# Exits of the mLSTM and RWKV stages inside their plans, and float32 products with 64 columns in column halves

## The chip, the cores and the metric

The kernel runs on one core of a Trainium2 chip. Its time is the device time of one execution in microseconds (us); of several runs the median counts. Engines: PE is TensorE, DVE is VectorE, ACT is ScalarE, POOL is GpSimd, SP issues most DMAs. A traced execution gives the times of single instructions, in us from the start of its span.

## The reference

A stack of four layers (mLSTM, RWKV7, Retention, mLSTM) on 256 tokens of width 1024; around each mixer stand two half-step SwiGLU networks:

```python
for layer in range(DEPTH):
    g = norm_g[layer]
    h = swiglu_ffn(rms_norm(x, g[0]), ffn_w_gu[layer, 0], ffn_w_down[layer, 0])
    x = x + HALF_STEP * rms_norm(h, g[1])
    h = mixer[layer % 3](rms_norm(x, g[2]), ...)
    x = x + rms_norm(h, g[3])
    h = swiglu_ffn(rms_norm(x, g[4]), ffn_w_gu[layer, 1], ffn_w_down[layer, 1])
    x = x + HALF_STEP * rms_norm(h, g[5])
```

mLSTM computes for each of 4 heads gated scores of q and k times v, normalises and gates the result y, and multiplies it by w_out. RWKV7 runs, per head of 64, the recurrence `S = S*w + (S a) b^T + v k^T`, `y = S r`, normalises y, adds `sum(r k r_k) v`, gates it and multiplies by w_out. All of it is float32.

## The kernel before

The 256 tokens are two tiles (t = 0, 1) of 128 partitions; x[0] and x[1] (in the order: x_88, x_89) stay in SBUF. The weights come as 345 units of 1 MB. Each unit is split into a high part (`hi`, copied by ACT, L127) and a low part (`lo`, subtracted by DVE or POOL, L135), and every dense product is three products at reduced precision, `hi*xh + lo*xh + hi*xl` (`mm3`, L334 to L340). This splitting is called prep below. So that the next units are ready, preps are put in between the other work of ACT, DVE and POOL.

The net is a row of twelve stages. A stage's body ends with its output products: `acc[t]` (two PSUM halves of 512 columns for each tile) adds up w_out's units times the transposed and split head outputs `hT`; a unit makes 12 products per tile (`down_steps`). Then come, for each tile, `residual` (ACT squares L268, DVE L270, a chain of small DVE operations for the reciprocal root, and x itself, L276) and `x_transpose` (8 PE transposes of x, L292; DVE scales them, L298; ACT makes `xh`, L299; DVE makes `xl`, L302), and then the next stage's first products, `head.mm`.

`boundary` writes this passage in a fixed order: the stage gives back a list `tail` of functions f(t); all f(0) go first, then preps and the residual of tile 0, then the f(1), with the x transposes of tile 0 ahead of the last of them, then the residual of tile 1 and `head.mm`. The mLSTM stage leaves the output products of heads 1 to 3 to the tail, with the transposes and splits (L1046, L1063, L1067) of heads 2 and 3; RWKV leaves those of its last two groups for tile 1.

The bodies of mLSTM and RWKV are put in order by `Plan`, a list scheduler that runs while the program is built. A body is a set of chains (Python generators) that yield an engine, a cost in ns, and whether a PSUM bank is taken. Plan takes the chain whose step can start first, after adding to each chain's time its constant from `PUT_OFF`; it assumes four PSUM banks and one port that DVE's two-input operations share with POOL. Nothing of this is decided on the chip: there every engine follows its own written order and waits on semaphores.

In RWKV, `solve` (L1959), `right` (L1826) and `outputs` (L2009, L2012, L2014) multiply float32 matrices of 128 x 128 by 64 moving columns (two in L2014), four products to a group. `by_rows` (L346) issues other small products in two halves of 64 partitions. `lora2` makes the second LoRA products for w and for a, each with 64 rows. `s.slot` and `s.heads` only choose slices.

## Time and profile before

| | us |
|---|---|
| median of 3 runs (lowest, highest) | 2175.19 (2174.14, 2177.9) |
| profiled execution | 2175.98 |
| its span | 2174.2 |
| mLSTM bodies and exits (about) | 196 to 327, 1860 to 1994 |
| RWKV | 660 to 956 |
| mean granted clock of PE | 0.983 |

A line of the trace's timeline gives start, length, engine, line of the program, operation, output and inputs (partitions x elements), a count, and in brackets the idle time of the engine before it and what ended it. Matmuls overlap, so the distance between two starts is the pitch of one, not its length. PEclk is the clock granted to PE, 1.0 being full.

### The profile page before, as it was taken

How to read it: one execution, taken by the hardware profiler on the slowest of the kernel's cores; microseconds unless marked ns; L12 is line 12 of the kernel's file. 1: busy time of each engine (PE TensorE's matmuls, PEld its weight loads, DVE VectorE, ACT ScalarE, POOL GpSimd, SP SyncE). 2: the span in 40 equal slices, each digit the busy share in tenths (PEclk: the TensorE clock that was granted, in tenths of full speed). 3: DMA queues.
4: the chain of work that ended last, by engine and by line, in shares of the span. 5: the costliest groups of instructions: out<-in, count | busy, mean ns of one | idle time of the engine just before them, and what ended most of it. 6: DMA issues, size and time to landing. Idle time of an engine off the chain costs nothing.

```text
span 2174.2 us, 38941 instructions
## 1 busy us (share of the span) xinstructions
PE 2091.4 (96%) x16136; PEld 1976.0 (91%) x16136; DVE 1492.2 (69%) x2234; ACT 1112.9 (51%) x1804; POOL 356.2 (16%) x615
## 2 busy tenths in 40 slices
PE   8999989999998999879999999999999999998998
PEld 8999879999997988879999999998999999887997
DVE  6766777667666787677677668556766766757765
ACT  5545655445445754345445445444544554655543
POOL 2001421002000466730001003211000100252000
PEclk9999999999999999889999999999999999999999
DMA  7553245555552320136546555554654555234651
GB/s 278 214 201 136 108 171 211 211 191 195 216 192 98 124 76 31 55 145 251 195 156 244 204 194 194 175 175 146 230 204 169 217 211 194 100 117 191 233 205 68
DMA packets 56226, 376.46 MB, mean 173 GB/s; under 512 B 7144, under 2 KB 8808, under 8 KB 11888
## 3 DMA queue, kind: packets, MB, share of 16 engines
q1 hardware_dynamic: 55472, 372.59, 46.9%
q8 instruction: 127, 2.08, 0.4%
q10 hardware_dynamic: 576, 1.38, 0.2%
q14 instruction: 51, 0.42, 0.1%
HBM read 372.89 MB, written 1.05 MB: 172 GB/s over the span
## 4 chain that ended last, share of the span: by engine, by line
PE 82%; DVE 11%; ACT 3%; issue 2%; POOL 1%; DMA 1%; DVEq 0%; SPq 0%; ACTq 0%; POOLq 0%
PE mm L338 14%; PE mm L340 14%; PE mm L339 14%; PE acc L336 7%; PE acc L334 7%; PE acc L335 7%; PE mm L334 4%; PE mm L335 4%; PE mm L336 4%; DVE lo L135 3%; DVE s L864 1%; ACT hi L127 1%; DVE s L270 1%; DVE x L276 1%; PE acc L1440 1%
## 5 line engine op out<-in xcount | busy, mean ns | idle before, releaser
L135 DVE TENSOR_TENSOR lo<-raw,hi 128x1024 fp32r<-128x1024 f32 (+1 forms) x700 | 810.3, 1200 | 188.6 <-ACT hi L127 186.2
L127 ACT ACTIVATE hi<-raw 128x1024 fp32r<-128x1024 f32 (+1 forms) x766 | 697.7, 964 | 116.5 <-issue 57.0
L338 PE MATMUL mm<-xh,hi 128*128 128x256 f32 x2688 | 743.1, 276 | 0.0
L339 PE MATMUL mm<-xl,hi 128*128 128x256 f32 x2688 | 741.3, 276 | 0.0
L340 PE MATMUL mm<-xh,lo 128*128 128x256 f32 x2688 | 741.2, 276 | 0.0
L339 PEld LDWEIGHTS mm<-xl,hi 128*128 128x128 f32 x2688 | 518.0, 193 | 1.7
L338 PEld LDWEIGHTS mm<-xh,hi 128*128 128x128 f32 x2688 | 518.0, 193 | 1.7
L340 PEld LDWEIGHTS mm<-xh,lo 128*128 128x128 f32 x2688 | 518.1, 193 | 0.0
L336 PE MATMUL acc<-hi,s 128*128 128x512 f32 x864 | 331.3, 383 | 7.4 <-DVE s L1067 6.3
L334 PE MATMUL acc<-hi,s 128*128 128x512 f32 x864 | 333.9, 387 | 4.3 <-ACT s L1063 2.3
L335 PE MATMUL acc<-lo,s 128*128 128x512 f32 x864 | 330.0, 382 | 0.0
L571 ACT ACTIVATE s<-s 128x256 f32<-128x256 f32 x152 | 63.6, 419 | 431.9 <-DVE s L569 431.9
L334 PE MATMUL mm<-hi,xh 128*128 128x256 f32 x960 | 268.8, 280 | 5.3 <-ACT xh L1392 5.3
L335 PE MATMUL mm<-lo,xh 128*128 128x256 f32 x960 | 265.4, 276 | 0.9 <-DVE lo L135 0.9
L336 PE MATMUL mm<-hi,xl 128*128 128x256 f32 x960 | 265.2, 276 | 0.0
L336 PEld LDWEIGHTS acc<-hi,s 128*128 128x128 f32 x864 | 164.9, 191 | 34.1 <-DVE s L1067 7.9
L252 POOL TENSOR_SCALAR rr_v<-ssx 128x1 f32<-128x1 f32 x22 | 5.2, 236 | 1148.7 <-ACT junk L307 1148.6
L334 PEld LDWEIGHTS mm<-hi,xh 128*128 128x128 f32 x960 | 185.5, 193 | 6.8 <-ACT xh L1392 5.6
L334 PEld LDWEIGHTS acc<-hi,s 128*128 128x128 f32 x864 | 165.2, 191 | 26.7 <-ACT s L1063 3.4
L335 PEld LDWEIGHTS mm<-lo,xh 128*128 128x128 f32 x960 | 185.4, 193 | 2.5 <-DVE lo L135 1.3
L336 PEld LDWEIGHTS mm<-hi,xl 128*128 128x128 f32 x960 | 185.4, 193 | 0.2 <-DVE xl L1394 0.2
L335 PEld LDWEIGHTS acc<-lo,s 128*128 128x128 f32 x864 | 165.2, 191 | 21.0
(408 smaller groups left out, 2206.5 us busy)
## 6 DMA issues: line engine op xcount, KB each, us to landing
raw<-in_w SPq DMA_DIRECT2D x345, 1024.0 KB, 4.8
s<-in_g_post SPq DMA_DIRECT2D x12, 512.0 KB, 5.9
x<-in_x ACTq DMA_DIRECT2D x2, 512.0 KB, 6.0
s<-in_rw_l SPq DMA_DIRECT2D x4, 256.0 KB, 6.1
s<-in_rw_ln SPq DMA_DIRECT2D x8, 128.0 KB, 4.2
out<-x SPq DMA_DIRECT2D x3, 256.0 KB, 2.1
s<-in_decay SPq DMA_DIRECT2D x1, 512.0 KB, 6.7
s<-in_rw_zmask SPq DMA_DIRECT2D x1, 320.0 KB
```

The costliest lines, as they stand in the source:

```text
L127: s.nc.scalar.activation(out=o[0], in_=src, func=AF.Copy)
L135: (e or s.nc.vector).tensor_tensor(out=o[1], in0=src, in1=o[0].bitcast(F32), op=ALU.subtract)
L270: nc.vector.tensor_tensor(out=hg[:, h, :], in0=acc[h], in1=g[:, h * 512:h * 512 + 512], op=ALU.mult)
L276: nc.vector.scalar_tensor_tensor(out=s.x[t][:, c], in0=hg[:, h, :], scalar=r, in1=s.x[t][:, c], op0=ALU.mult, op1=ALU.add)
L334: mm(out, ah, wh, start=first, stop=False)
L335: mm(out, ah, wl, start=False, stop=False)
L336: mm(out, al, wh, start=False, stop=last)
L338: mm(out, wh, ah, start=first, stop=False)
L339: mm(out, wh, al, start=False, stop=False)
L340: mm(out, wl, ah, start=False, stop=last)
L571: nc.scalar.activation(out=sg, in_=gn[:, 0, :], func=AF.Silu)
L864: nc.vector.scalar_tensor_tensor(out=c[:, g, :], in0=x[:, g, j:j + T], scalar=s.cw[:, 4 * g + h, j:j + 1], in1=c[:, g, :], op0=ALU.mult, o ...
```

## The change

The x transposes become a chain that Plan can run (`x_transpose_steps`). The plans of mLSTM and RWKV go on to the end of the stage: `dense` (in RWKV `out`) makes the products of tile 0 for all units, a new chain `out1` those of tile 1, and a new chain `leave` the residual of tile 0 and its x transposes. All head outputs are transposed and split within the plan. The bodies give back an empty tail, and `boundary` goes directly to the residual of tile 1 and `head.mm`. `by_cols` issues each float32 product with 64 (or 2) moving columns as two halves of 64 stationary columns, which write partitions 0 to 63 and 64 to 127. The two LoRA chains become one that alternates between the two row halves. Costs and the tables `PUT_OFF` of both stages change.

```diff
-    def x_transpose(s, t, gi):
+    def x_transpose(s, *a):
+        for _ in s.x_transpose_steps(*a):
+            pass
+
+    def x_transpose_steps(s, t, gi):
...
         for h in range(2):
+            yield "pe", 450.0, True
             pt = s.mm()
             for q in range(4):
                 k = 4 * h + q
                 nc.tensor.transpose(pt[:, q * P:(q + 1) * P], s.x[t][:, k * P:(k + 1) * P], s.ident)
...
+    def by_cols(s, out, w, x, start=True):
+
+        for h in range(2):
+            c = slice(64 * h, 64 * h + 64)
+            s.nc.tensor.matmul(out[c], w[:, c], x, start=start, stop=True, skip_group_check=True)
...
     def boundary(s, tail, acc, gpost_i, factor, head):
...
+        if not tail:
+            s.parts_ahead(s.n_get + NHEAD)
+            s.begin_next(acc, gpost_i, factor, head)
+            return
         for f in tail:
             f(0)
...
+    def leave(s, *after):
+
+        n = s.n
+        yield [("acc", 0)]
+        yield from n.residual_steps(0, s.acc[0], s.gi, 1.0)
+        if after:
+            yield list(after)
+        yield from n.x_transpose_steps(0, s.gi + 1)
...
-    PUT_OFF = dict(conv=325, gates=300, attend=50, evacs=125, prep=375, prep_po=575, dense=150)
+    PUT_OFF = dict(conv=700, gates=675, attend=200, evacs=975, prep=475, prep_po=1050, dense=750, out1=825, leave=0)
...
+        for h in range(1, s.H):
+            yield from s.need(len(s.ORDER) + h)
+            s.units[h] = n.get()
+            s.plan.mark("u", h)
+            yield [("hT", h)]
+            yield from n.down_steps(s.units[h], s.hT[h], 0, s.acc[0], False, h == 3)
+        s.plan.mark("acc", 0)
+
+    def out1(s):
+
+        for h in range(1, s.H):
+            yield [("u", h), ("hT", h)]
+            yield from s.n.down_steps(s.units[h], s.hT[h], 1, s.acc[1], False, h == 3)
+            s.n.free()
...
-            if h < 2:
-                yield "pe", 430.0, True
-                pt = s.trans_mm(h)
...
+            yield "pe", 430.0, True
+            pt = s.trans_mm(h)
...
-        us = [n.get() for _ in range(3)]
-
-        def f(t, i):
-            if i > 1 and t == 0:
-                s.trans(i)
-            n.down(us[i - 1], s.hT[i], t, s.acc[t], False, i == 3)
-        return [lambda t, i=i: f(t, i) for i in (1, 2, 3)], s.acc
+        return [], s.acc
...
-    PUT_OFF = dict(enter0=500, enter1=450, tail=825, small=150, lora1=275, borrows=250, mix1=50, mix0=200, inv0=50,
+    PUT_OFF = dict(enter0=575, enter1=725, tail=775, small=600, lora1=975, borrows=425, mix1=425, mix0=375, inv0=275,
...
-    def lora2(s, i):
+    def lora2(s):
...
-        rows = slice(64 * i, 64 * i + 64)
+        rows = [slice(64 * i, 64 * i + 64) for i in range(2)]
         for g in range(4):
-            yield "pe", 640.0, True
-            ps = n.mm()
+            yield "pe", 640.0, 2
+            ps = [n.mm() for _ in range(2)]
             for j in range(2):
                 c = slice(D + (2 * g + j) * P, D + (2 * g + j + 1) * P)
-                n.mm3(ps[:, j * T:(j + 1) * T], hi[rows, c], lo[rows, c], s.la[0][rows], s.la[1][rows], True, True, False, False)
...
+                for p, (w, x) in enumerate(((0, 0), (0, 1), (1, 0))):
+                    for i, r in enumerate(rows):
+                        nc.tensor.matmul(ps[i][:, j * T:(j + 1) * T], s.l2[w][r, c], s.la[x][r], start=p == 0, stop=p == 2)
...
-            yield "pe", 870.0, c == 0
+            yield "pe", 620.0, c == 0
...
-                nc.tensor.matmul(ps[:, c, i, :], Aak()[:, s.slot(c, i), :], s.heads(c, g)[:, i, :], start=True, stop=True)
+                n.by_cols(ps[:, c, i, :], Aak()[:, s.slot(c, i), :], s.heads(c, g)[:, i, :])
...
-                yield "pe", 870.0, True
+                yield "pe", 650.0, True
...
-                    mm(ps[:, i, :], AT[:, s.slot(c, i), :], U[:, i, :], start=True, stop=True)
+                    n.by_cols(ps[:, i, :], AT[:, s.slot(c, i), :], U[:, i, :])
...
-                    mm(Y[:, i, :], m[:, i % 2, 1, i // 2, :], V[:, i, :], start=c == 0 and i == 0, stop=False, skip_group_check=True)
-                yield "pe", 1100.0
+                    n.by_cols(Y[:, i, :], m[:, i % 2, 1, i // 2, :], V[:, i, :], c == 0 and i == 0)
+                yield "pe", 820.0
                 for i in range(4):
-                    mm(Y[:, i, :], m[:, i % 2, 0, i // 2, :], U[:, i, :], start=False, stop=True, skip_group_check=True)
+                    n.by_cols(Y[:, i, :], m[:, i % 2, 0, i // 2, :], U[:, i, :], False)
                 for j in range(2):
-                    mm(ps[:, 256 + 2 * j:258 + 2 * j], v["rk"][:, j, c * P:(c + 1) * P], s.rkb[:, 2 * g + j, :], start=False, stop=True, skip_group_check=True)
+                    n.by_cols(ps[:, 256 + 2 * j:258 + 2 * j], v["rk"][:, j, c * P:(c + 1) * P], s.rkb[:, 2 * g + j, :], False)
...
-            for t in range(2):
-                if g < 2 or t == 0:
-                    yield [("hT", g, t)]
...
+            s.plan.mark("u", g)
+            yield from n.down_steps(s.units[g], s.hT[g], 0, s.acc[0], g == 0, g == 3)
+        s.plan.mark("acc", 0)
+
+    def out1(s):
+
+        for g in range(4):
+            yield [("u", g), ("hT", g, 1)]
+            yield from s.n.down_steps(s.units[g], s.hT[g], 1, s.acc[1], g == 0, g == 3)
+            s.n.free()
...
+            out1=s.out1(), leave=s.leave(("U", 3, 1), ("R", 3, 1)))
...
-        def f(t, g):
-            if t == 1:
-                if g == 3:
-                    s.trans(3, 1)
-                n.down(s.units[g], s.hT[g], 1, s.acc[1], False, g == 3)
-        return [lambda t, g=g: f(t, g) for g in (2, 3)], s.acc
+        return [], s.acc
```

The order of the instructions moves at many places. Three of them follow. Names end in a number of their own in either program; mm and acc are PSUM, xh and xl the split x.

PE at the start of the first mLSTM's scores, before: L924 and L925 transpose the gates, L946 to L950 are products of the gates, mm_2616 (L338 to L340) are q/k products of heads that come later, of which 12 stand between, and L993 makes the first scores.

```order
L924 MATMUL mm_2570<-ident,s_2394 128x4
L925 MATMUL mm_2570<-ident,s_2395 128x4
...
L946 MATMUL acc_2598<-causal_94,ident_95 128x128
...
L947 MATMUL acc_2598<-s_2575,s_1166 128x384
L948 MATMUL acc_2598<-s_2576,s_1166 128x384
L950 MATMUL acc_2599<-s_2559 128x256
...
L338 MATMUL mm_2616<-xh_2054,hi_2481 128x256
L339 MATMUL mm_2616<-xl_2055,hi_2481 128x256
L340 MATMUL mm_2616<-xh_2054,lo_2482 128x256
...
L993 MATMUL acc_2632<-s_2233,s_2610 128x256 x3
L997 MATMUL acc_2633<-ones,s_2610 128x1 x3
```

After (all lines lie some tens further down):

```order
L973 MATMUL mm_2572<-ident,s_2394 128x4
L974 MATMUL mm_2572<-ident,s_2395 128x4
...
L348 MATMUL mm_2578<-xh_2064,hi_2464 128x256
L349 MATMUL mm_2578<-xl_2065,hi_2464 128x256
L350 MATMUL mm_2578<-xh_2064,lo_2465 128x256
...
L995 MATMUL acc_2641<-causal_94,ident_95 128x128
...
L996 MATMUL acc_2641<-s_2594,s_1166 128x384
L997 MATMUL acc_2641<-s_2595,s_1166 128x384
L999 MATMUL acc_2642<-s_2629 128x256
...
L348 MATMUL mm_2578<-xh_2064,hi_2464 128x256
...
L1042 MATMUL acc_2675<-s_2233,s_2668 128x256 x3
L1046 MATMUL acc_2676<-ones,s_2668 128x1 x3
```

36 instead of 0 of the q/k products stand between the gates' transposes and the gates' products, and 12 as before between those and the scores.

PE at the first mLSTM's exit, before: acc_3203 and acc_3204 are tile 0, acc_3205 and acc_3206 tile 1, hi_3305 is the last unit, and mm_3508 is the next stage's first product.

```order
L1046 MATMUL mm_3348<-ident,s_3297 128x128 x4
L334 MATMUL acc_3203<-hi_3305,s_3353 128x512
...
L336 MATMUL acc_3204<-hi_3305,s_3354 128x512
L334 MATMUL acc_3205<-hi_3180,s_3001 128x512
...
L336 MATMUL acc_3206<-hi_3180,s_3002 128x512
L334 MATMUL acc_3205<-hi_3248,s_3330 128x512
...
L336 MATMUL acc_3206<-hi_3248,s_3331 128x512
L292 MATMUL mm_3438<-ident,x_88 128x128 x4
...
L334 MATMUL acc_3205<-hi_3305,s_3353 128x512
...
L336 MATMUL acc_3206<-hi_3305,s_3354 128x512
L334 MATMUL mm_3508<-hi_3371,xh_3436 128x256
```

After: acc_3172 and acc_3173 are tile 0, acc_3174 and acc_3175 tile 1, hi_3298 is the last unit.

```order
L344 MATMUL acc_3175<-hi_3132,s_3062 128x512
...
L346 MATMUL acc_3174<-hi_3251,s_3243 128x512
L1094 MATMUL mm_3362<-ident,s_3359 128x128 x4
L344 MATMUL acc_3174<-hi_3251,s_3242 128x512
...
L346 MATMUL acc_3175<-hi_3251,s_3243 128x512
L344 MATMUL acc_3172<-hi_3298,s_3367 128x512
...
L346 MATMUL acc_3173<-hi_3298,s_3368 128x512
L344 MATMUL acc_3174<-hi_3298,s_3367 128x512
...
L346 MATMUL acc_3175<-hi_3298,s_3368 128x512
L295 MATMUL mm_3459<-ident,x_88 128x128 x4
...
L344 MATMUL mm_3528<-hi_3384,xh_3470 128x256
```

Behind tile 0's last product stand 12 instead of 24 products of tile 1 ahead of the transposes of x_88, and none instead of 12 between these and the next stage.

PE at RWKV's exit, before: L2009 to L2014 are the last outputs, L2104 transposes the heads' results of tile 0 and then of tile 1, and acc_10195 and acc_10196 are tile 1.

```order
L2009 MATMUL mm_10404<-q_7419,s_10298 128x64 x4
L2012 MATMUL mm_10404<-s_10311,s_10298 128x64 x4
L2014 MATMUL mm_10404<-rw_rkb_6423,s_8373 128x2 x2
L334 MATMUL acc_10193<-hi_9988,s_10296 128x512
...
L2104 MATMUL mm_10450<-ident,s_10323 128x128 x2
L334 MATMUL acc_10193<-hi_10320,s_10453 128x512
...
L334 MATMUL acc_10195<-hi_9988,s_10296 128x512
...
L336 MATMUL acc_10196<-hi_9988,s_10297 128x512
L292 MATMUL mm_10550<-ident,x_88 128x128 x4
...
L2104 MATMUL mm_10567<-ident,s_10323 128x128 x2
L334 MATMUL acc_10195<-hi_10320,s_10453 128x512
...
L334 MATMUL mm_10621<-hi_10390,xh_10548 128x256
```

After: acc_10360 and acc_10361 are tile 1, L362 is `by_cols`.

```order
L2045 MATMUL mm_10646<-s_10538,s_9402 128x128 x2
L362 MATMUL mm_10646<-q_7442,s_10532 64x64 x8
L362 MATMUL mm_10646<-s_10579,s_10532 64x64 x8
L362 MATMUL mm_10646<-rw_rkb_6441,s_8395 64x2 x4
L344 MATMUL acc_10358<-hi_10407,s_10632 128x512
...
L346 MATMUL acc_10359<-hi_10407,s_10633 128x512
L2142 MATMUL mm_10736<-ident,s_10509 128x128 x2
L295 MATMUL mm_10740<-ident,x_88 128x128 x4
...
L344 MATMUL acc_10360<-hi_10407,s_10632 128x512
...
L346 MATMUL acc_10361<-hi_10407,s_10633 128x512
L344 MATMUL mm_10823<-hi_10541,xh_10750 128x256
```

The 12 products of tile 1 (hi_9988) that stood ahead of the transposes of x_88 have gone ahead of the last outputs.

DVE at the same place, before: L2089 finishes the heads' results of tile 1, L135 are preps, and L270 to L276 the residual of tile 0.

```order
L2087 TENSOR_TENSOR s_10324<-s_10324,s_10444 128x256
L2089 TENSOR_TENSOR s_10323<-s_10324,s_10446 128x256
L135 TENSOR_TENSOR lo_10500<-raw_10448,hi_10499 128x1024 x2
L135 TENSOR_TENSOR lo_10508<-raw_10467,hi_10507 128x1024 x2
L270 TENSOR_TENSOR s_10516<-acc_10193,s_10197 128x512
...
L250 TENSOR_SCALAR rr_v_10522<-ss_10515 128x1
...
L240 TENSOR_SCALAR res_r_10521<-nr_y_955_10524 128x1
L276 SCALAR_TENSOR_TENSOR x_88<-s_10516,res_r_10521,x_88 128x512 x2
L298 TENSOR_TENSOR s_10560<-mm_10550,gpre 128x512
```

After: L2076 to L2127 finish the results, L270 to L276 are the residual.

```order
L2076 TENSOR_TENSOR s_10510<-mm_10646,rw_st_10511 128x256
...
L270 TENSOR_TENSOR s_10694<-acc_10358,s_10362 128x512
...
L206 TENSOR_SCALAR nr_y_951_10705<-rw_st_10511 128x4
L270 TENSOR_TENSOR s_10694<-acc_10359,s_10362 128x512
...
L250 TENSOR_SCALAR rr_v_10712<-ss_10693 128x1
...
L2123 TENSOR_TENSOR s_10510<-s_10510,rw_rs_10704 128x256
L240 TENSOR_SCALAR res_r_10709<-nr_y_955_10714 128x1
...
L276 SCALAR_TENSOR_TENSOR x_88<-s_10694,res_r_10709,x_88 128x512
L2127 TENSOR_TENSOR s_10509<-s_10510,s_10642 128x256
L276 SCALAR_TENSOR_TENSOR x_88<-s_10694,res_r_10709,x_88 128x512
...
L304 TENSOR_TENSOR s_10752<-mm_10740,gpre 128x512
...
L135 TENSOR_TENSOR lo_10771<-raw_10658,hi_10770 128x512 x2
```

The residual is mixed with the finishing, and the four low halves that stood between them are gone from there. SP's rows (the DMAs) are as many in both programs.

More of the change, by code (lines that the diff above doesn't have):

```diff
@@ L293, in x_transpose @@
             pts.append(pt.rearrange("p (q c) -> p q c", q=4))
+        if t == 0:
+            s.xh, s.xl = s.new_x()
         xg = s.sc(4, [NK, P])
@@ L297, in x_transpose @@
             g = s.gpre[:, gi * NK + 4 * h:gi * NK + 4 * h + 4, None].to_broadcast([P, 4, P])
+            yield "vp", 600.0
             nc.vector.tensor_tensor(out=xg[:, k, :], in0=pts[h], in1=g, op=ALU.mult)
+            if s.plan:
+                s.plan.drop()
+            yield "ac", 520.0
             nc.scalar.activation(out=s.xh[:, k, c], in_=xg[:, k, :], func=AF.Copy)
@@ L458, in boundary, with begin_next @@
         s.parts_ahead(upto)
+        s.begin_next(acc, gpost_i, factor, head)
+    def begin_next(s, acc, gpost_i, factor, head):
         s.residual(1, acc[1], gpost_i, factor)
         s.x_rstd(0)
-        s.prep(upto)
+        s.prep(s.n_get + NHEAD)
         for i in range(NHEAD):
@@ L1029, in attend @@
             s.plan.mark("y", h)
-            if h < 2:
-                yield "pe", 430.0, True
-                pt = s.trans_mm(h)
-                s.hT[h] = [n.sc(2, [2, T], F32R) for _ in range(2)]
-                for engine, step in s.split_g(h, pt):
-                    yield engine, 660.0
-                    step()
-                s.plan.drop()
-                s.plan.mark("hT", h)
+            yield "pe", 430.0, True
+            pt = s.trans_mm(h)
+            s.hT[h] = [n.sc(2, [2, T], F32R) for _ in range(2)]
+            for engine, step in s.split_g(h, pt):
+                yield engine, 660.0
+                step()
+            s.plan.drop()
+            s.plan.mark("hT", h)
     def trans_mm(s, h):
@@ L1047, in trans_mm @@
         return pt
-    def trans(s, h):
-        n = s.n
-        pt = s.trans_mm(h)
-        s.hT[h] = [n.sc(2, [2, T], F32R) for _ in range(2)]
-        for _, step in s.split_g(h, pt):
-            step()
     def split_g(s, h, pt):
@@ L1074, in body @@
         s.base = n.n_get
-        chains = dict(conv=s.conv(), gates=s.gates2(), attend=s.attend(), evacs=s.evacs(), prep=preps[0], prep_po=preps[1], dense=s.dense())
+        chains = dict(conv=s.conv(), gates=s.gates2(), attend=s.attend(), evacs=s.evacs(), prep=preps[0], prep_po=preps[1], dense=s.dense(),
+                      out1=s.out1(), leave=s.leave())
         s.plan.run(chains, s.PUT_OFF, preps)
-        us = [n.get() for _ in range(3)]
-        def f(t, i):
-            if i > 1 and t == 0:
-                s.trans(i)
-            n.down(us[i - 1], s.hT[i], t, s.acc[t], False, i == 3)
-        return [lambda t, i=i: f(t, i) for i in (1, 2, 3)], s.acc
+        return [], s.acc
 class Retention(Stage):
@@ L2107, in trans_mm @@
         return pt, [h[:, :, t * P:(t + 1) * P] for h in s.hT[g]]
-    def trans(s, g, t):
-        pt, hT = s.trans_mm(g, t)
-        s.n.split(hT, pt)
     def transposes(s, t):
@@ L2136, in out @@
             s.units[g] = n.get()
-            for t in range(2):
-                if g < 2 or t == 0:
-                    yield [("hT", g, t)]
-                    if g + t == 0:
-                        s.acc = n.new_acc()
-                        n.load_gpost(s.gi)
-                    yield from n.down_steps(s.units[g], s.hT[g], t, s.acc[t], g == 0, g == 3)
-            if g < 2:
-                n.free()
+            yield [("hT", g, 0)]
+            if g == 0:
+                s.acc = n.new_acc()
+                n.load_gpost(s.gi)
+            s.plan.mark("u", g)
[6 more added lines that the diff above has]
+            s.n.free()
     def body(s):
```

37 lines of the change are left out of this document (17 added, 20 removed).

## Prediction

> **What bounds the kernel now.** I read the page first: the share of each engine, then the chain of work that ended last.
>
> ```profile
> PE 2091.4 (96%) x16136; PEld 1976.0 (91%) x16136; DVE 1492.2 (69%) x2234; ACT 1112.9 (51%) x1804; POOL 356.2 (16%) x615
> PE 82%; DVE 11%; ACT 3%; issue 2%; POOL 1%; DMA 1%; DVEq 0%; SPq 0%; ACTq 0%; POOLq 0%
> ```
>
> TensorE (PE) is busy for 2091.4 of 2174.2 us, so only 83 us are idle, and the chain that decides the end lies on it. Time can come from three places: PE's idle time, PE's work, and stretches in which PE ran at half the granted clock. To place them I took the table of windows (us from the start, length, PE busy, then the other engines, PEclk) over the first mLSTM body and its exit, RWKV, and the second mLSTM, and over the stretches of low clock in them.
>
> ```profile
> 677.00:924.50 247.50, 224.71 (x2233) 205.48 (x2232) 181.66 (x358) 143.87 (x345) 135.49 (x173) 0.94 0.19 68
> 226.00:327.00 101.00, 87.14 (x555) 77.29 (x554) 70.67 (x138) 54.98 (x112) 37.11 (x80) 0.92 0.38 141
> 1860.00:1994.00 134.00, 118.87 (x854) 109.11 (x852) 94.33 (x181) 77.02 (x148) 46.68 (x103) 0.96 0.38 138
> 231.41:241.65 10.24, 9.29 (x38) 8.46 (x37) 6.87 (x14) 7.37 (x16) 3.47 (x9) 0.50 0.58 205
> 299.68:306.51 6.83, 5.50 (x15) 4.08 (x15) 1.11 (x3) 0.53 (x2) 0.00 (x0) 0.50 0.69 285
> 890.19:903.84 13.65, 12.38 (x76) 11.20 (x77) 5.60 (x13) 4.25 (x11) 9.65 (x21) 0.50 0.01 3
> 937.97:951.62 13.65, 6.84 (x21) 5.45 (x22) 9.42 (x21) 3.20 (x9) 0.00 (x0) 0.50 0.41 150
> ```
>
> PE idles 13.9 us of the first mLSTM window, 15.1 us of the second and 22.8 us of RWKV's body. Half of PE's busy time in a stretch at clock 0.50 is loss: 9.29/2 + 5.50/2 = 7.4 us in the first mLSTM, 12.38/2 = 6.2 us and 6.84/2 = 3.4 us in RWKV. The waits of PE in the first mLSTM window (who waited for what: us, times, longest) say which idle time is whose:
>
> ```profile
> PE acc L336 <- DVE s L1067: 3.2, 2, 3.0
> PE acc L993 <- DVE s L981: 2.7, 2, 1.8
> PE mm L292 <- DVE x L276: 2.5, 2, 1.7
> PE mm L993 <- ACT s L842: 1.8, 1, 1.8
> ```
>
> L993 is the heads' score products, which wait for the gates' DVE work; L336 is an output product that waits for the split of a head's output (L1067), and L292 is the next stage's transposes, which wait for the residual (L276).
>
> **The change, part by part.**
>
> *mLSTM.* At stake in the first are 13.9 + 7.4 = 21.3 us. In the new order 36 q/k products stand between the gates' small transposes and the first scores, so that the scores' waits (L993, 2.7 + 1.8) and the stretch at 231.41 lose their cause: the gates' DVE and ACT work is covered by 36 x 0.11 = 4 us of PE work. The later heads' scores then wait in part (about 1 us each for two heads, estimated from the 1.8 us above). All four heads' outputs are split in the plan, so the 3.0 us at L336 go too. What comes instead is read from the exit, PE first, then DVE and ACT (start, length):
>
> ```profile
> 309.44 0.38 PE L336 MATMUL acc<-hi,s 128*128 128x512 f32 x1
> 309.65 0.38 PE L334 MATMUL acc<-hi,s 128*128 128x512 f32 x1
> 314.62 0.38 PE L336 MATMUL acc<-hi,s 128*128 128x512 f32 x1
> 316.68 1.23 PE L292 MATMUL mm<-ident,x 128*128 128x128 f32 x8 [1.68 <-DVE x L276]
> 317.66 0.46 PE L334 MATMUL acc<-hi,s 128*128 128x512 f32 x1
> 320.33 0.27 PE L334 MATMUL mm<-hi,xh 128*128 128x256 f32 x1
> ```
> ```profile
> 312.34 1.28 DVE L270 TENSOR_TENSOR s<-acc,s 128x512 f32<-128x512 f32 x2
> 315.78 1.42 DVE L276 SCALAR_TENSOR_TENSOR x<-s,res_r,x 128x512 f32<-128x512 f32 x2
> 318.24 1.28 DVE L298 TENSOR_TENSOR s<-mm,gpre 128x512 f32<-128x512 f32 x2
> ```
> ```profile
> 318.96 1.23 ACT L299 ACTIVATE xh<-s 128x512 fp32r<-128x512 f32 x2 [5.42 <-DVE s L298]
> ```
>
> The last product of tile 0 is the one at 309.44; 24 products of tile 1 follow (309.65 to 314.83, 0.216 each), then 1.68 us of waiting, the transposes, and 12 more products that cover the way from the transposes to the first product of the next stage at 320.33. In the new order only 12 products of tile 1 follow tile 0's last (2.6 us), and none stands behind the transposes. The residual takes DVE from 312.34 to 316.5 for the first half of x (4.2 us) and starts about 0.3 us after the last product, so the transposes wait 4.5 - 2.6 = 1.9 us. From the transposes' end to the first product it took 317.66 - 320.33 with cover; without cover PE waits for L298, xh and xl, some 3 us with two of the next units' halves between them on DVE. That is 4.9 us of idle time in the place of 1.7. It buys one thing: residual 1 starts earlier against the next stage's products, so its 0.8 us (2.5 - 1.7) falls to about 0.2. My count of the new waits is 0.8 (gates' transposes) + 0.6 (gates' products) + 2.0 (later scores) + 0.5 (the last head's transposes) + 4.9 + 0.2 = 9.0 us, plus 1.8 us for a low-clock stretch that the exit brings (a 3.0 us wait brought 6.83 us at half clock here; PE would be busy for about 3.6 of them), plus 2.4 us because POOL takes whole low halves that DVE's small operations then share a port with (bounds 0 and 4). 13.2 against 21.3: a gain of 8 us, bounds 4 and 12. The second mLSTM has the same waits, 1.2 us more idle, and less at half clock (134 x 0.04 = 5.4 us of clock against 101 x 0.08 = 8.1): 7. **Together -15.** Nothing is added to SP's queue, and its rows keep their order.
>
> The Trainium skill ("TensorE: Matmul & The Clock Gate", "Why this matters for your kernels") says that no PE gap may be longer than about 3 us, since one idle window brings the clock back to half. By it the exit's 1.9 and 3 us, with only 1 us of transposes between, cost the low clock each time; the trace's 3.0 us gap before 299.68 agrees, its 1.68 us gap does not bring it. The sum has it in once, at 1.8.
>
> *RWKV's exit.* PE, then DVE, then ACT:
>
> ```profile
> 924.51 0.56 PE L2014 MATMUL mm<-rw_rkb,s 128*128 128x2 f32 x4
> 924.93 0.46 PE L334 MATMUL acc<-hi,s 128*128 128x512 f32 x1
> 934.77 0.38 PE L336 MATMUL acc<-hi,s 128*128 128x512 f32 x1
> 943.49 1.94 PE L292 MATMUL mm<-ident,x 128*128 128x128 f32 x8 [8.35 <-DVE x L276]
> 952.04 0.27 PE L334 MATMUL mm<-hi,xh 128*128 128x256 f32 x1
> ```
> ```profile
> 934.23 0.42 DVE L2089 TENSOR_TENSOR s<-s,s 128x256 f32<-128x256 f32 x1
> 934.58 4.67 DVE L135 TENSOR_TENSOR lo<-raw,hi 128x1024 fp32r<-128x1024 f32 x4
> 942.59 1.42 DVE L276 SCALAR_TENSOR_TENSOR x<-s,res_r,x 128x512 f32<-128x512 f32 x2
> ```
> ```profile
> 937.71 0.58 ACT L268 ACTIVATE junk<-acc 128x512 bf16<-128x512 f32 x1
> ```
>
> From the last of the recurrence's products (924.93) to the next stage's first product (952.04) pass 27.1 us. The output y(3,1) is done at 934.65. The residual of tile 0 does not need y(3,1); it starts late because four low halves (4.67 us) and ACT's high halves are queued ahead of its squares (937.71). The new order interleaves the finishing of y(3,1) and the residual on DVE without those preps: y at about 9.4 us (9.7 now), transposes done at 11.3, first product at 14 to 16.5 with 12 products between. Of the 45 products now behind 924.93, 21 (4.5 us) go ahead of it. Gain 27.1 - 4.5 - 16 = 6.6, **-7**, bounds 3 and 9 (9 if the 13.65 us at half clock go with the 8.35 us wait, 3 if y is 4 us later).
>
> *Column halves.* None of the trace's products has column halves. Three rows are near: a whole-array group, groups of 64-row halves with 128 columns, and L2014 above.
>
> ```profile
> 785.57 1.04 PE L1959 MATMUL mm<-s,q 128*128 128x64 f32 x8
> 786.45 0.28 PE L1866 MATMUL acc<-gx,q 128*128 128x64 f16 x4
> ...
> 883.45 0.71 PE L346 MATMUL mm<-gx 64*128 64x128 f32 x8
> 884.10 0.40 PE L1879 MATMUL acc<-gx 128*128 128x128 f16 x4
> ...
> 884.76 1.17 PE L346 MATMUL mm<-s,gx 64*128 64x128 f32 x16
> 885.86 0.29 PE L1866 MATMUL acc<-gx,gx 128*128 128x64 f16 x4
> ```
>
> Four products of 64 moving columns are 8 instructions in 0.88 us, 0.11 each; L2014 with 2 moving columns takes 0.42/4 = 0.105 each, so the loading of 128 stationary columns sets the time, not the 64 moving ones. Row halves take 0.65 us for 8 and 1.10 for 16: 0.056 each, in pairs side by side, and 0.20 us to go in and out. A group now is 16 instructions that load half as many columns. Low end: pairs side by side at half of row halves' step, 16 x 0.028 + 0.20 = 0.65 us, a gain of 0.23. High end: one behind the other at a whole load each, 16 x 0.11 + 0.20 = 1.96, a loss of 1.1. I take the low end, because the row halves are the nearest row and do run side by side. There are 40 such groups (16 in the solve, 8 in right, 16 in the outputs): 40 x 0.23 = 9.2, and the two-column products gain at most 8 x 0.2 less a part of an entry, +-1. Interleaving the two LoRA halves saves at most 3 steps of 0.115 in each of 4 groups, 1.4. Of these 11 us RWKV's PE is busy for 224.71 of 247.50, and in the solve chain it is waited for by DVE; I let 0.7 of it reach the end: **-8**.
>
> The Trainium skill ("TensorEngine Tiling (Array Packing)", "Key Properties") has different tiles load and multiply in parallel, and a drain at every change of mode; the 0.20 us above would be that drain. By the Trainium skill ("TensorE: Matmul & The Clock Gate", "Part 3: Packing small matmuls — row/col tiling") loads overlap running products only where the row group differs. Column halves share it, and no run here shows them; that is the second rival.
>
> *The order inside RWKV.* All delays are new and the plan comes out with the inverse chains' last product at the same place of PE's order. The 22.8 us idle and 6.2 us at half clock there can shrink or grow; without a row for either I take **0**, bounds -12 and +12.
>
> Sum: -15 - 7 - 8 = -30. The profiled execution took 2175.98 us, 1.8 outside the span; 2146.0 by it, and 0.8 less against the median 2175.19: **2145 us**.
>
> **Rivals.**
> 1. *RWKV's own order gains too.* Its waits are many and short, which an order can fill. A half of 22.8 and the 6.2 us at half clock: -30 - 11.4 - 3 = -44, 2131 us.
> 2. *Column halves do not load side by side.* Then a group takes 16 x 0.055 + 0.20 = 1.08 us, 0.2 more than now: +8 instead of -8 (less the LoRA's 1): -15, 2160 us. For it speaks that both halves need all 128 rows; against it, only the likeness to row halves.
> 3. *They load a whole array's time each.* 1.96 us a group, +1.08 x 40 = +43, all of it on PE: -22 + 43 = +21, 2196 us. It decides against the change from 0.55 us more a group (22/40), that is from 1.43 us. L2014's 0.105 us for two columns speaks for a price that does not fall with the moving columns; the LDWEIGHTS would have to keep its price though it loads half the columns.
> 4. *The exits without cover take back what the bodies gain.* 3 us more idle and 3.4 us instead of 1.8 lost to the clock at both mLSTM exits (2 x 4.6, so -15 becomes -6) and RWKV's y 4 us late (-7 becomes -3): -17, 2158 us. The exits above, where the wait in front of a bare stretch is followed by the low clock, speak for it; that DVE holds fewer preps there, against.
> 5. *The plan's order loses inside RWKV.* The joined LoRA step takes two of the plan's four PSUM banks at once, and a solve step that wants one waits; if that and the moved starts make the 22.8 us idle half as long again (11 us), the sum is -19, 2156 us. No row speaks for it but the number of short waits.
>
> **How the numbers follow.** Forecast 0.40 (its own range 2138 to 2152), rival 1 0.16, rival 2 0.12, rival 3 0.07, rival 4 0.10, rival 5 0.15. The range from 2128 to 2166 leaves out rival 3 and tails of some 0.12. A measurement of this kernel tells 0.2% (4.4 us) from no change. Only rival 3 and a sum of rivals 2, 4 and 5 (0.05) come out at or beyond it: faster 0.87, same 0.04, slower 0.09.
>
> **What would show it.** The mLSTM window: no wait of L993's kind over 1.1 us, no half clock before the scores, and two waits at the exit, about 1.9 us before the transposes and about 3 us behind them. RWKV's exit: about 16 us from the last two-column product to the next stage's first product, no single wait over 4 us. The split products: 16 instructions of 64 columns in about 0.65 us; at 1.1 us rival 2 holds, at 1.4 us or more rival 3. Wrong above all would be the price of the column halves, which no row shows, and the body of RWKV, whose order I only count as even.

## The result, and the profile after

The changed kernel takes 2161.55 us (median of 4, 2160.51 to 2162.96) against 2176.18 for the kernel before: 14.6 us less, a ratio of 0.9936 with an interval of 0.9923 to 0.9948. The forecast was 30 us. The direction and the range held; the size is a little under half. The profiled execution took 2162.96 us, its span 2161.2. Below are the page's first line, then windows (us, length, PE busy, other engines, PEclk): the two that answer to the bodies of RWKV and of the first mLSTM, and four stretches at half clock. The first two of these stretches lie in the first mLSTM and at its exit, the other two late in RWKV's body, where three earlier ones of 6.83 us are not shown.

```profile
PE 2076.1 (96%) x16488; PEld 1959.1 (91%) x16488; DVE 1486.7 (69%) x2243; ACT 1119.2 (52%) x1830; POOL 375.4 (17%) x628
672.06:927.78 255.72, 222.10 (x2612) 194.88 (x2610) 185.25 (x361) 145.72 (x350) 150.26 (x182) 0.92 0.20 70
225.40:320.50 95.10, 83.39 (x540) 75.55 (x540) 69.66 (x144) 57.77 (x121) 40.37 (x83) 0.91 0.41 147
267.63:274.46 6.83, 6.83 (x29) 6.21 (x28) 6.83 (x12) 5.97 (x11) 2.84 (x2) 0.50 0.43 152
308.59:318.83 10.24, 6.75 (x28) 5.68 (x28) 10.15 (x14) 5.12 (x11) 4.74 (x7) 0.50 0.61 218
885.44:895.68 10.24, 8.62 (x61) 6.86 (x59) 3.46 (x9) 3.23 (x8) 8.84 (x19) 0.50 0.40 155
919.58:929.82 10.24, 7.73 (x75) 6.53 (x75) 6.76 (x15) 2.71 (x6) 9.40 (x10) 0.50 0.32 114
```

PE is busy for 15.3 us less (2091.4 - 2076.1) and idle for 85.1 us instead of 82.8. So the kernel gained by PE's shorter work; the idle time, from which most of the forecast was to come, did not fall. RWKV's body (from its first wait for a transpose to the last output) idles 33.6 us instead of 22.8.

To see it by stage, cut each trace at the first product of every stage (here from the network ahead of RWKV to the first product behind RWKV, before and changed):

```profile
499.31:952.04 452.73, 417.90 (x3631) 387.52 (x3630) 324.55 (x579) 239.47 (x490) 154.66 (x201) 0.95 0.35 128
494.37:942.34 447.97, 408.21 (x3984) 372.12 (x3983) 317.58 (x574) 238.00 (x491) 164.94 (x207) 0.95 0.35 127
```

With the stage behind added to each, since the second residual reaches into it, and with half of PE's busy time at clock 0.50 taken as loss:

| us | length | PE work at full clock | lost to half clock | PE idle | forecast |
|---|---|---|---|---|---|
| first mLSTM | 309.4 to 304.9 (-4.5) | -1.7 | 7.4 to 6.8 | 14.4 to 12.2 | -8 |
| RWKV | 630.5 to 627.8 (-2.7) | -11.8 | 14.5 to 17.0 | 34.8 to 41.4 | -15 |
| second mLSTM | 307.4 to 302.1 (-5.3) | -1.7 | 5.0 to 3.6 | 15.3 to 13.0 | -7 |

The work of each mLSTM stage fell by 1.7 us, which the forecast had at nothing; no run here takes this apart. The column halves did what was forecast. A group in the changed kernel, and the ones in a row with the two-column products (start, length):

```profile
901.92 0.69 PE L362 MATMUL mm<-s,q 128*64 128x64 f32 x16
902.54 0.48 PE L344 MATMUL acc<-hi,s 128*128 128x512 f32 x1
...
906.39 0.69 PE L362 MATMUL mm<-q,s 128*64 128x64 f32 x16
906.90 0.64 PE L362 MATMUL mm<-s,s 128*64 128x64 f32 x16
907.37 0.35 PE L362 MATMUL mm<-rw_rkb,s 128*64 128x2 f32 x8
907.65 0.38 PE L2022 MATMUL mm<-s,s 128*128 128x128 f32 x1
```

0.62 us alone and 0.47 to 0.51 within a run of halves, against 0.88; the two-column products 0.28 against 0.42.

At the first mLSTM's exit, PE, then DVE, then POOL:

```profile
308.48 1.00 PE L295 MATMUL mm<-ident,x 128*128 128x128 f32 x4 [2.49 <-DVE x L276]
310.15 1.09 PE L295 MATMUL mm<-ident,x 128*128 128x128 f32 x4 [0.68 <-DVE x L276]
313.00 0.58 PE L344 MATMUL mm<-hi,xh 128*128 128x256 f32 x1 [1.76 <-ACT xh L308]
314.85 0.58 PE L346 MATMUL mm<-hi,xl 128*128 128x256 f32 x1 [1.06 <-DVE xl L312]
```
```profile
307.00 3.01 DVE L276 SCALAR_TENSOR_TENSOR x<-s,res_r,x 128x512 f32<-128x512 f32 x2
309.93 1.75 DVE L135 TENSOR_TENSOR lo<-raw,hi 128x512 fp32r<-128x512 f32 x1
```
```profile
300.86 10.28 POOL L135 TENSOR_TENSOR lo<-raw,hi 128x512 fp32r<-128x512 f32 x7 [5.44 <-ACT hi L127]
```

Four waits of 6.0 us together, where 4.9 were forecast. While POOL makes seven low halves (300.86 to 311.14), the last step of DVE's residual takes 3.01 instead of 1.42 us and a low half of DVE's own 1.75 instead of about 0.7. The clock is at half for 10.24 us from there on, three periods of 3.41 where the forecast had two.

In RWKV's tail, PE, then DVE, then POOL:

```profile
915.18 0.69 PE L362 MATMUL mm<-s,q 128*64 128x64 f32 x16 [0.47 <-ACT s L1992]
919.89 0.37 PE L2005 MATMUL mm<-s,q 128*128 128x64 bf16 x4 [4.02 <-DVE s L2001]
927.32 0.54 PE L362 MATMUL mm<-rw_rkb,s 128*64 128x2 f32 x8
937.27 0.66 PE L2142 MATMUL mm<-ident,s 128*128 128x128 f32 x2 [5.64 <-DVE s L2127]
942.34 0.27 PE L344 MATMUL mm<-hi,xh 128*128 128x256 f32 x1
```
```profile
896.45 1.20 DVE L2134 TENSOR_TENSOR s<-s,q 128x512 f32<-128x512 f32 x1 [6.24 <-POOL s L2132]
897.68 0.42 DVE L2001 TENSOR_TENSOR s<-mm,s 128x256 bf16<-128x256 f32 x1
...
915.08 1.20 DVE L227 SCALAR_TENSOR_TENSOR nr_y<-nr_u,nr_y 128x4 f32<-128x4 f32 x1
916.31 1.18 DVE L220 TENSOR_TENSOR nr_u<-nr_y 128x4 f32<-128x4 f32 x1
917.53 1.19 DVE L222 TENSOR_TENSOR nr_u<-nr_u,rw_st 128x4 f32<-128x4 f32 x1
```
```profile
914.99 3.71 POOL L135 TENSOR_TENSOR lo<-raw,hi 128x512 fp32r<-128x512 f32 x3
918.66 0.72 POOL L1999 TENSOR_TENSOR s<-s,s 128x256 f32<-128x256 f32 x1
```

The exit itself came out as worked out: from the last two-column product (end 927.78) to the next stage's first product 14.6 us (14 to 16.5 forecast), though with one wait of 5.64 us where none over 4 was to show. But that last product came late. Counted from the first product of the network ahead, it ended at 425.6 before and at 433.4 in the changed kernel; with the halves' 8 us less and the 4.5 us of moved products more, 422 was forecast. The lines show two causes to test: the last group's solve (L1999 on POOL, L2001 on DVE) is queued behind the finishing of the third group (L2132, L2134) and behind low halves, and DVE's operations on 4 columns take 1.2 instead of 0.16 us while POOL makes low halves.

### The profile page after: what moved, and what is told of

The parts are those of the page before. It is cut to its first block, busy times and chain, and to the rows that moved or that the text cites. A ratio compares the mean times of both kernels' runs of the same rounds, so it can differ in the third digit from the quotient of the medians.

```text
span 2161.2 us, 39698 instructions
## 1 busy us (share of the span) xinstructions
PE 2076.1 (96%) x16488; PEld 1959.1 (91%) x16488; DVE 1486.7 (69%) x2243; ACT 1119.2 (52%) x1830; POOL 375.4 (17%) x628
## 4 chain that ended last, share of the span: by engine, by line
PE 81%; DVE 9%; ACT 4%; POOL 3%; issue 2%; DMA 1%; DVEq 0%; POOLq 0%; SPq 0%; ACTq 0%
PE mm L348 14%; PE mm L350 14%; PE mm L349 14%; PE acc L344 7%; PE acc L346 7%; PE acc L345 7%; PE mm L346 4%; PE mm L344 4%; PE mm L345 4%; DVE lo L135 2%; ACT hi L127 2%; PE mm L362 1%; DVE x L276 1%; DVE s L270 1%; POOL lo L135 1%
## 5 line engine op out<-in xcount | busy, mean ns | idle before, releaser
L135 DVE TENSOR_TENSOR lo<-raw,hi 128x1024 fp32r<-128x1024 f32 (+1 forms) x709 | 801.6, 1170 | 190.5 <-ACT hi L127 188.8
L344 PEld LDWEIGHTS mm<-hi,xh 128*128 128x128 f32 x960 | 188.6, 196 | 11.8 <-ACT xh L1429 6.0
```

The costliest lines, as they stand in the source:

```text
L135: (e or s.nc.vector).tensor_tensor(out=o[1], in0=src, in1=o[0].bitcast(F32), op=ALU.subtract)
L344: mm(out, ah, wh, start=first, stop=False)
```

## The experiments

The kernel before was timed again beside each group of kernels: 2175.47 us beside the first four, 2175.71 beside ml_hold12, ml_old_exit, ml_old_table and rw_no_pool_tail, 2175.38 beside solve3_first, rw_old_table and rwkv_only, and 2174.67 beside the last three.

**The parts alone: A (the halves are worth their work, RWKV's order took it back) against B (RWKV hides them).**

`cols_only`, the kernel before with

```diff
-                    mm(ps[:, i, :], AT[:, s.slot(c, i), :], U[:, i, :], start=True, stop=True)
+                    n.by_cols(ps[:, i, :], AT[:, s.slot(c, i), :], U[:, i, :])
...
```

> The kernel before with column halves alone: every engine keeps its order, only the float32 products with 64 (or 2) moving columns are issued in halves. Theory A: the halves are worth about what they take from PE's work (12 us in the trace of the changed kernel), of which 0.7 or more reach the end in the old order too: 2164 to 2168 us; the changed kernel lost the rest through its new order in RWKV. Rival B: RWKV waits for chains through DVE, ACT and POOL, and shorter products only lengthen PE's waits: 2171 us or more, whatever the order.

`after_whole`:

```diff
-        for h in range(2):
-            c = slice(64 * h, 64 * h + 64)
-            s.nc.tensor.matmul(out[c], w[:, c], x, start=start, stop=True, skip_group_check=True)
+        s.nc.tensor.matmul(out, w, x, start=start, stop=True, skip_group_check=True)
```

> The changed kernel with whole products in the place of the column halves, all orders kept. Theory A: 8 to 12 us more than the changed kernel (2170 to 2174). Rival B: at most 4 more (2165 or less).

`mlstm_only` and `mlstm_cols` (whole class exchanged):

```diff
-class Rwkv(Stage):   # changed
+class Rwkv(Stage):   # of before; in mlstm_cols with the edit of cols_only
```

> The changed kernel with RWKV's class as before (order, tail, whole products): only the mLSTM stages changed. From the trace of the changed kernel, by the lengths of the two mLSTM stages and of the first part of the stages behind them (-4.5 and -5.4): 10 us less than before, 2166. If the mLSTM part is worth the 15 that were forecast and the stages' lengths mislead: 2161.

> The changed mLSTM, RWKV in its old order with column halves. Theory A: the two add up, 2156 to 2158, faster than the changed kernel by 4 us. Rival B: as mlstm_only, 2164 or more.

| | us | ratio to before (interval) |
|---|---|---|
| cols_only | 2168.53 | 0.9965 (0.9952 to 0.9977) |
| after_whole | 2176.44 | 1.0008 (0.9998 to 1.0018) |
| mlstm_only | 2169.62 | 0.9975 (0.9965 to 0.9984) |
| mlstm_cols | 2159.82 | 0.9929 (0.9917 to 0.9942) |

Halves: 6.9 us in RWKV's old order with the old mLSTM (A had 7 to 11, B at most 4), 9.8 with the changed mLSTM (mlstm_cols against mlstm_only), and 14.9 in the new order (A had 8 to 12), where without them the kernel is no faster than before. B falls. In the traces of the last pair, after_whole and the changed kernel, RWKV's stage and the one behind it are 11.3 us shorter with halves: 12.5 us of work and 0.8 of clock loss less, 2.0 of idle time more. Another 1.9 us lie in the second mLSTM, whose instructions stand in the same order in both kernels, but which lost 6.7 us to half clock without halves and 3.6 with them.

mLSTM alone: 5.9 us with whole products (10 expected), 8.7 with halves. In mlstm_only's trace both mLSTM stages are as short as in the changed kernel; RWKV, in the order of before on every engine, takes 3.5 us longer than before, with 17.6 instead of 14.5 us lost to half clock. And mlstm_cols, with RWKV's old order, old exit and old LoRA, takes 1.7 us less than the changed kernel (4 expected): beside the halves, all that the change does in RWKV gains nothing, and with whole products it costs 6.8 us (after_whole against mlstm_only).

**mLSTM: the body's order, the exit, the place of the cover.** `ml_hold12`:

```diff
-            yield [("u", h), ("hT", h)]
+            yield [("u", h), ("hT", h)] + [("xT",)] * (h == 3)
```

with a mark xT behind the transposes of x[0].

> The changed kernel; in both mLSTM stages the last unit's 12 products of tile 1 stand behind the x transposes instead of ahead of them. Nothing else moves on any engine. Theory A (the cover is the same 2.6 us wherever it stands, idle time only moves): the wait ahead of the transposes grows from 2.5 to about 5, the two behind them (1.8 and 1.1) go, sum even: 2159 to 2163 us. Rival B (the waits behind the transposes keep the clock low into the next stage, so the cover is worth more there): 3 us less at half clock per mLSTM, 2154 to 2157.

2162.73 us, in theory A's range. At the first exit the long wait stands ahead of the transposes:

```profile
306.69 1.09 PE L295 MATMUL mm<-ident,x 128*128 128x128 f32 x4 [5.04 <-DVE x L276]
```

One of 0.59 us stands between their two halves and none behind them: 5.6 us, against 6.0. In this trace the first mLSTM stage lost 1.9 us to half clock instead of 6.8 and is 2.2 us shorter, as B's reason would have it; the second is not shorter. Since that loss also moves by this much between kernels in which the stage is the same (last section), the trace does not decide it, and the time of the whole is A's. `ml_old_exit` and `ml_old_table`:

```diff
# ml_old_exit: mLSTM class of before with the new table
-    PUT_OFF = dict(conv=325, gates=300, attend=50, evacs=125, prep=375, prep_po=575, dense=150)
+    PUT_OFF = dict(conv=700, gates=675, attend=200, evacs=975, prep=475, prep_po=1050, dense=750)
# ml_old_table: changed class with the old one
+    PUT_OFF = dict(conv=325, gates=300, attend=50, evacs=125, prep=375, prep_po=575, dense=150, out1=825, leave=0)
```

> The changed kernel with the mLSTM class as before, tail and all, but the new table of constants: the body's new order alone. If the mLSTM gain (about 10 us in the stages' lengths) comes from the body (scores covered by q/k products): 2160 to 2163. If it comes from the exit inside the plan: 2168 or more.

> The changed kernel with the mLSTM's constants of before for the chains that were there (out1 and leave keep theirs): the exit inside the plan alone. If the gain comes from the exit: 2160 to 2163; if from the body's order: 2168 or more.

2172.38 (0.9982, 0.9973 to 0.9991) and 2171.51 (0.9984, 0.9974 to 0.9994): each lies where the other part was to explain the gain. Of an mLSTM stage's 816 instructions on PE, the first 708 stand in the changed order in ml_old_exit, and the first 684 in the old one in ml_old_table. `rwkv_only`, with neither part (the mLSTM class of before), takes 2168.44 (below). So neither the body's order nor the exit alone gains anything (both are 3 to 4 us slower than with neither), and both together gain 6.9 us. The expectations had treated the parts as a sum.

**RWKV's tail.** `rw_no_pool_tail`, in the changed kernel's preps:

```diff
+            if ("U", 3, 0) in s.plan.marks:
+                e = None      # DVE in POOL's place
```

> The changed kernel; from the first tile's solution of RWKV's last group on, POOL takes no more low halves, DVE does them. The order up to there is the same. Theory A (in the tail POOL's low halves stand ahead of the solve's POOL subtraction and slow DVE's small operations from 0.16 to 1.2 us): the 4.0 us wait at the solve shrinks to about 1, 2156 to 2158. Rival B (the tail is a chain whose length the engines' shares do not set, or DVE is as late with the halves of its own): 2160 to 2164.

2166.91 us (0.9961, 0.9948 to 0.9973), 5.4 more than the changed kernel and above both ranges: theory A fails in this form. DVE now has four low halves (3.02 us) ahead of the solve's L2001, which comes as late as before; the plan also put the residual ahead of the last finishing. `solve3_first`:

```diff
-solve3=625
+solve3=100
```

> The changed kernel with one constant of RWKV's plan, solve3, at 100 instead of 625: the solve of the last head group goes ahead of the finishing of the third group's results (five POOL products of 512 columns, L2132, and DVE's L2134 that waits for them) and of POOL's low halves. The order is the same up to PE's row 6894 of the first 7123. Theory C (the changed order loses in RWKV's tail, because the last solve's subtractions on POOL and DVE are queued behind work that nothing waits for): the last outputs come some 10 us earlier, behind them stand 84 output products as cover, RWKV's idle time falls from 41 to about 33 us, 2151 to 2155. Rival D (the loss lies ahead of the tail, where the solves start 17 us later than in the old order): 2160 to 2164.

2163.25 us (0.9946, 0.9934 to 0.9959): no gain, in D's range, though C's first half came true. The last outputs end at 905.6 instead of 927.8, with 75 output products behind them instead of 24. Counted from the first product of the network ahead, that is 412.9 instead of 433.4. The 51 products that changed sides take 0.216 us each, 11.0 together; so with as many products behind it the recurrence would end 9.5 us earlier than in the changed kernel, at about 424 (an estimate), where 422 was forecast. D's reason falls too: the first solve starts 301.4 us behind that first product, as late as in the changed kernel (302.6; before: 285.4). PE then waits here (PE, DVE, POOL):

```profile
923.24 0.69 PE L2142 MATMUL mm<-ident,s 128*128 128x128 f32 x2 [5.97 <-DVE s L2127]
```
```profile
913.66 1.79 DVE L135 TENSOR_TENSOR lo<-raw,hi 128x512 fp32r<-128x512 f32 x1
915.38 1.25 DVE L2117 TENSOR_SCALAR rw_st<-rw_st 128x4 f32<-128x4 f32 x1
916.66 1.19 DVE L206 TENSOR_SCALAR nr_y<-rw_st 128x4 int32<-128x4 int32 x1
...
920.32 0.16 DVE L225 SCALAR_TENSOR_TENSOR nr_u<-nr_u 128x4 f32<-128x4 f32 x1
```
```profile
913.62 6.65 POOL L135 TENSOR_TENSOR lo<-raw,hi 128x512 fp32r<-128x512 f32 x5 [0.67 <-ACT hi L127]
```

Five low halves on POOL end at 920.27, and with them DVE's slow operations. Three more kernels are `rw_old_table` (RWKV's constants of before in the changed class), `rwkv_only` (the mLSTM class of before) and `before_again` (the kernel before once more); the edit of the first, in part:

```diff
-                   solve1=400, solve2=250, solve3=625, outputs=600, ...
+                   solve1=250, solve2=225, solve3=325, outputs=375, ...
```

> The changed kernel with RWKV's constants of before for the chains that were there (the joined LoRA chain takes w's, out1 and leave keep theirs): the exit inside the plan, halves and joined LoRA with the old delays. Theory C: the last solve (solve3 325, finish 250 as before) runs ahead of its cover again, 2152 to 2158. Rival D: also 2152 to 2158, since solves start early again; what tells them apart is where they lie in the trace. If the new constants themselves are worth something: 2164 or more.

> The changed kernel with the mLSTM class as before, constants and all: RWKV's change alone. If the parts add up (mLSTM 5 to 9 us by the two pairs of kernels so far): 2167 to 2171.

> The kernel before once more, for its profile: how much PE loses to half clock in RWKV and in the mLSTM stages from one execution to the next. If those losses hang on the order alone: 14.5 us in RWKV, 7.4 and 5.0 in the mLSTM stages, as in the first profile. If they hang on where the kernel meets the clock's periods: other values by some us, as all changed kernels showed 17 to 19.6 in RWKV.

rw_old_table: 2183.8 us (1.0041, 1.0027 to 1.0055), neither C nor D (2152 to 2158), but in the range of the third case (2164 or more). Its RWKV idles 52.1 us and loses 27.2 to half clock. The old constants do not suit the new set of chains; nothing can be read from them on solve3 alone. rwkv_only: 2168.44 (0.9972, 0.9961 to 0.9983), as expected. before_again's profile has the same losses to half clock in RWKV (14.3 against 14.5) and in the first mLSTM (7.4 both), and 7.4 instead of 5.0 in the second. That two executions of one kernel agree does not show that the order alone sets the loss; the last section compares more kernels.

**Which is it, POOL's low halves or the place of the cover?** `quiet_ml` and `s3_quiet` (the latter also with solve3=100):

```diff
+            if any(m in s.plan.marks for m in (("hT", 3),)):                # quiet_ml
+            if any(m in s.plan.marks for m in (("hT", 3), ("U", 3, 1))):    # s3_quiet
+                e = None
```

> The changed kernel; in both mLSTM stages, once the last head's output is split, POOL makes no more low halves, DVE makes them. PE's order does not move. Theory E (POOL's seven low halves at the exit stretch DVE's residual, L276 from 1.4 to 3.0 us and L135 from 0.7 to 1.75, and that is 2 to 3 us of the exit's idle time): L276 at 1.4 us again, the exit's waits fall from 6.0 to about 4 us in each mLSTM stage, 2157 to 2159. Rival F (DVE pays the same for making them itself, four of them ahead of the residual): the waits ahead of the transposes stay or grow, 2161 to 2164.

> The kernel with solve3 at 100, and POOL without low halves from the split of the last mLSTM head's output on, and in RWKV from the last solution on. Theory E: the finishing of RWKV's last results, stretched there by POOL's low halves (small DVE operations at 1.2 instead of 0.16 us), takes 5 us less, the 6.0 us wait at its transposes falls to 1 or 2; with 2 us from each mLSTM exit 2151 to 2155. Rival F: 2160 to 2164, the idle time is as long and lies elsewhere.

`s3_quiet_hold` adds the edit of ml_hold12 in both stages.

> The same, with the last unit's 12 products of tile 1 behind the x transposes in mLSTM and RWKV. If cover is worth the same wherever it stands: as s3_quiet, within 3 us. If less low clock at the exits counts: 3 to 6 less.

| | us | ratio to before (interval) |
|---|---|---|
| quiet_ml | 2160.46 | 0.9940 (0.9927 to 0.9954) |
| s3_quiet | 2155.64 | 0.9913 (0.9900 to 0.9927) |
| s3_quiet_hold | 2154.80 | 0.9909 (0.9896 to 0.9923) |

In quiet_ml, with PE's order untouched, the residual is as fast as before:

```profile
305.68 1.41 DVE L276 SCALAR_TENSOR_TENSOR x<-s,res_r,x 128x512 f32<-128x512 f32 x2
```

The four waits of 6.0 us at the first exit become 2.5 + 1.1 + 1.1 = 4.7. E has the mechanism, but DVE's own low halves ahead of the residual keep the first wait at 2.5, and the time fell by 1.1 us, within the intervals and between the ranges of E and F. In s3_quiet, PE's wait at RWKV's last transposes and one of the small operations of DVE that lead to it (two lines lower in its code than above):

```profile
923.81 0.44 PE L2144 MATMUL mm<-ident,s 128*128 128x128 f32 x2 [1.92 <-DVE s L2129]
```
```profile
920.69 0.16 DVE L222 TENSOR_TENSOR nr_u<-nr_u,rw_st 128x4 f32<-128x4 f32 x1
```

1.92 us instead of the 5.97 of solve3_first, and 0.16 instead of 1.2. s3_quiet takes 5.9 us less than the changed kernel (4.4 less, if each is set against the kernel before that was timed beside it); it lies just above E's range, and the two intervals still touch (0.9923 and 0.9927). Between the two traces, 4.8 us apart, RWKV's stage and the one behind it are 5.1 us shorter, all of it idle time (36.3 us instead of 41.4), and the two mLSTM stages together take as long as in the changed kernel. s3_quiet_hold is 6.8 us faster than the changed kernel, with intervals that meet only at 0.9923. Against s3_quiet it moves by 0.8 us: within what these runs can tell, cover is worth the same on either side of the transposes. It is the fastest version found.

## Where the prediction failed, and what held

**RWKV, where it failed.** "The order inside RWKV ... I take 0", and with it the forecast of that stage, -7 and -8. The halves gave their 12 us of work, and the exit took the 14.6 us that were worked out, but the recurrence ended 11 us later than the sum had it (433.4 against 422), and RWKV's body idles 10.8 us more. The runs show in place of the 0: the solve of the last group stands behind other work. Put ahead of that (solve3_first), it gives back 9.5 of the 11 us by the estimate above, but no time, because PE then waits 6.0 us for the finishing that POOL's low halves stretch. With POOL's low halves gone from there too (s3_quiet), that wait is 1.9 us and RWKV's idle time falls by 5.1.

The prediction's 6.2 us at half clock in RWKV's body before were too few: the trace has two more stretches of 6.83 us there, at 681.97 and 869.71, and 11.1 us lost. Rival 5 had the place and the size, 11 us more idle time in the body; it was given 0.15. Its mechanism, two banks for the joined LoRA step, no run tests by itself. The order rows of the front part showed the exit, not where the last solve stands against the finishing of the third group. A part stays open: in s3_quiet RWKV's stage is 7.8 us shorter than before, of 15 forecast, and no run shows what holds the rest.

**mLSTM**, forecast -15: -9.8 by the traces (3.4 of it work that the sum did not have), 5.9, 8.7 and 6.9 in three pairs of kernels. The step that failed is the loss to half clock, forecast at 1.8 us in the first stage and measured at 6.8. The waits came out nearly as counted: 9.0 us and the 2.4 set aside for POOL's low halves are 11.4, and the trace has 11.6: 1.2 at the gates' transposes (0.8 forecast), none at the gates' products (0.6), 1.6 and 1.0 at later scores (2.0, and none over 1.1), 1.8 at a head's transposes (0.5), 6.0 at the exit and the products behind it (4.9). The 2.4 are among these: 1.6 us at L276 and 1.1 at a low half ahead of L304. The small operations of that exit, which were to pay, did not (last section).

Of the 6.8 us at half clock 3.4 lie at the exit, in three periods instead of two, and 3.4 in the stretch at 267.63, which begins 1.0 us behind the end of the 1.8 us wait. (The 3.0 us wait that the prediction puts before the stretch at 299.68 lasted until 300.45, so that stretch began within it.) How far this hangs on the order is open: with the same instructions in the same order on every engine this stage lost 3.3 us in solve3_first's trace and 3.6 in that of mlstm_cols.

**What held.** The price of the column halves, taken from the row halves: 0.65 forecast, 0.62 alone. Rivals 2 and 3 fall: halves that share all 128 rows take 0.62 us for 16 instructions, where one load after another at 0.055 (half of a whole load's 0.11, an estimate) would take 0.88 and more. So a rule that the Trainium skill has in "TensorE: Matmul & The Clock Gate" ("Part 3: Packing small matmuls — row/col tiling"), that loads overlap running products only where the row group differs, does not fit these rows. They agree with the Trainium skill's "TensorEngine Tiling (Array Packing)" ("Key Properties"), where different tiles load and multiply in parallel. Of the exit in RWKV, y at 9.3 us behind the last product (9.4 forecast) and the transposes' end at 11.5 (11.3) held too. Of the halves' 11 us, 0.7 was to reach the end; in RWKV's old order 6.9 and 9.8 did, 0.6 and 0.9.

Rival 4 (exits without cover take the gain back) is half true: the bare exits of the two mLSTM stages cost waits of 6.0 and 6.8 us, and a low clock at each. ml_hold12's time shows that moving the cover does not cure it. The reading that fits ml_old_exit and ml_old_table, argued and not shown, is that an exit lacks work that waits for nothing, and that the body uses the same work.

## What to carry to other kernels

A step moved past a wait carries cover with it: count the independent work of the whole stage once, and see which wait is left bare, rather than add up the waits that go. When a planner's order changes, look up, on every engine's queue, what the longest serial chain now stands behind; then look at the wait that comes next, since here moving the last solve alone only moved the wait to the finishing. Work given to a second engine "because it is idle" must be kept off the stretches in which short dependent operations of its neighbour are on the path; handing it back to that neighbour ahead of the same chain cost more still (rw_no_pool_tail).

## What the runs showed of the hardware

Operations of DVE on 4 columns take 0.16 us, and 1.18 to 1.25 us while POOL makes low halves of 512 columns at 1.24 to 1.33 us each. In solve3_first four of them in a row (915.38 to 920.28) each end 0.01 to 0.03 us behind one of POOL's low halves (916.60, 917.83, 919.05, 920.27): each waits for about one POOL instruction. The Trainium skill ("SBUF — State Buffer", "SBUF: two separate sides") calls the port that the two share an exclusive lock, held for a whole instruction, and the trace agrees. Not every small operation waits. L206 on 4 columns, which reads one small operand only, took 1.19 us; on one column, at the first mLSTM's exit in the changed kernel and beside POOL's seven low halves, it took this:

```profile
305.00 0.15 DVE L206 TENSOR_SCALAR nr_y<-rr_v 128x1 int32<-128x1 int32 x1
```

The other operations on one column around it take 0.15 to 0.27 us, as they do where POOL is idle. No run here shows why 4 columns wait and one does not.

Column halves of one 128-row operand run side by side: 16 instructions in 0.62 us with the entry and exit, 0.47 to 0.51 us each group when groups of halves follow one another, so going in and out costs about 0.11 to 0.15 us here (an estimate from the difference).

The losses to half clock do not hang on the order of work alone. In the changed kernel and in solve3_first the first mLSTM stage has the same instructions in the same order on PE, DVE, ACT and POOL, and PE waits 1.80 us just ahead of this window in both; the granted clock in it (the column of 0.50 and 1.00) is another (changed kernel, then solve3_first):

```profile
267.63:274.46 6.83, 6.83 (x29) 6.21 (x28) 6.83 (x12) 5.97 (x11) 2.84 (x2) 0.50 0.43 152
267.63:274.46 6.83, 5.64 (x40) 4.96 (x38) 6.83 (x12) 5.97 (x11) 2.82 (x2) 1.00 0.45 152
```

RWKV in the order of before lost 14.5, 14.3 and 17.6 us (before, before_again, mlstm_only); in the changed order it lost 13.8 to 20.7 us in six kernels (quiet_ml the least, rwkv_only the most). So a few us between two single traces that lie in this loss are not yet an effect of a change.
